# A bidirectional DeltaNet scan in two bursts a step, with split-off diagonal blocks and a written VectorE order

## Chip, core and metric

The kernel runs on one core of a Trainium2 chip. TensorE, VectorE (DVE in the rows), ScalarE (ACT), GpSimd (POOL) and the DMA queues of SyncE (SP), ScalarE and GpSimd work side by side. What counts is the device time of one execution in microseconds (us).

## What is computed

One layer of an encoder on 1024 tokens of width 1024: adaLN, one wide projection, attention beside a bidirectional gated DeltaNet, a merge, and an expert-choice MoE. The change lies in the DeltaNet. Each of its 8 heads cuts the sequence into 16 chunks of 64 tokens, builds a triangular matrix per chunk, inverts it, and scans the chunks forwards and, with other gates, backwards:

```python
L = jnp.where(strict, jnp.einsum('bhncd,bhnsd->bhncs', kb, k) * decay, 0.0)
T = lax.linalg.triangular_solve(eye + L, jnp.broadcast_to(eye, L.shape), left_side=True, lower=True,
                                unit_diagonal=True)
...
def step(state, inp):
    u_n, w_n, a_n, qg_n, kd_n, gl_n = inp
    v_new = u_n - w_n @ state
    o_n = qg_n @ state + a_n @ v_new
    state = state * gl_n[..., None, None] + jnp.einsum('bhck,bhcv->bhkv', kd_n, v_new)
    return state, o_n
```

## The kernel before

The stages follow each other: start and projections of the DeltaNet (to 217 us), matrices of the chunks (`dn_tile`), inversion (`dn_invert`), scan (`scan`, to about 758 us), attention, merge, router and MoE. Wide projections that nothing waits for are spread over the DeltaNet stages to keep TensorE busy: six `qkv_group`s, sixteen gate groups and four `dz` groups, each of 48 matmuls of 128x512 (fp32r, two halves of the operands multiplied in three passes). Their weights are loaded by the GpSimd queue, cast to `wh` by ScalarE (L272) and split to `wl` by VectorE (L273).

**Order.** The builder puts each engine's instructions in an order of its own: it goes by the written order as priority, by when it expects operands to be there, and by which of the buffers of a name (`tr` and `dn` in PSUM, two each; `wh`, `wl`, two each) is free. Inside `manual_schedule(engines={DVE})` VectorE's instructions keep the written order. Before, each of the 31 rounds of the inversion has such a block of its own, so splits and sums may stand between rounds wherever the builder puts them.

**Tiles of a chunk.** `dn_tile(j)` makes, for chunks 2j and 2j+1 and both directions, `at` and `nn` (128x512). `nn` goes to `n_d` in DRAM as 64x64 matrices. `dn_blocks` reads the two 32x32 diagonal blocks of each matrix back into `nb` (one row of 128 partitions for each chunk and head), in rows of 128 bytes and on ScalarE's queue (L508), for tiles 0 to 3 after tile 5 and for the rest after tile 7.

**Inversion.** `dn_invert` needs all of `nb`. It runs 31 rounds of two multiplies (L533) and two subtractions (L537) on VectorE, cut into eight parts between which eight projection groups are written; the blocks' inverses go to `w_d`. In the loop over the groups, `proj_ahead` is called for the next group ahead of the current group's `proj`, and overwrites the entry that this `proj` looks for, so all but the last of these groups load and split their weights twice.

**Scan.** In step t the forward direction treats chunk t, the backward one chunk 15-t; they lie in opposite halves of the 128 partitions. `scan_load` fetches a step's operands, `scan_merge` makes the missing off-diagonal 32x32 block of the inverse (products `pq`, L606, and `pr`, L612, 32x32 matmuls, one quadrant per direction), and `scan_step` does: `pk` (L626, key and query against the state, 128x128), `x = v - pk` on VectorE, `pv` (L638, 64x64 matmuls with the inverse), two scalings to `vb` and `va`, `pu` (L653, the state's update, 64x64), the sum on VectorE and two copies on ScalarE into the state `St`, and `po` (L663, 64x64, the output). A logical fp32 matmul is two instructions in the profile, so a product of 8 heads and two directions is 32. Between these pieces `fill(n)` writes n matmuls of the late projections (L1147, 48 ahead of the first merge). In steps 0 to 7 `attn_prep` (transposes on TensorE, normalisation and rotation on VectorE) runs beside.

Of the kernel before, what the change touches and what calls it, by code (L numbers as in the profile page):

```python
# [20 lines left out]
NT = 8  # L21
# [11 lines left out]
FILL = 12, 10, 4, 4, 8, 48  # L33
# [40 lines left out]
def rev(ap):  # L74

    *dims, (step, n) = [list(x) for x in ap.ap]
    return bass.AP(tensor=ap.tensor, offset=ap.offset + step * (n - 1), ap=dims + [[-step, n]])


class K:  # L80
# [274 lines left out]
    def dn_gates(self, ps):  # L355
# [71 lines left out]
        for t in range(16):  # L427
            for d in range(2):
                n = t if d == 0 else 15 - t
                nc.gpsimd.tensor_copy(gls[:, t, d * 4:d * 4 + 4], gl[:, n // 2, n % 2, d * 4:d * 4 + 4])  # L430
        self.eg, self.gls, self.dk = eg, gls, dk

    def dn_scalars(self):
# [13 lines left out]
        for t in range(16):  # L447
            for d in range(2):
                n = t if d == 0 else 15 - t
                j, x = divmod(n, 2)  # L450
                rows = slice(64 * x, 64 * x + 64)
                nc.gpsimd.tensor_copy(bs[rows, t, 0, :], b2[rows, j, d, :])
                nc.gpsimd.tensor_copy(bs[rows, t, 1, :], b2d[rows, j, d, :])
# [13 lines left out]
    def dn_tile(self, j):  # L467
# [13 lines left out]
        for d in range(2):  # L481
# [17 lines left out]
            for x in range(2):  # L499
                nc.sync.dma_start(self.n_d[d, 2 * j + x].rearrange("h s c -> s h c"),  # L500
                                  nn[64 * x:64 * x + 64].rearrange("p (h c) -> p h c", c=64))

    def dn_blocks(self, j0, j1):

        for d in range(2):
            src = self.n_d[d, 2 * j0:2 * j1].rearrange("n h (b s) c -> (n h) b s c", b=2)
            for b in range(2):
                self.nc.scalar.dma_start(self.nb[d][16 * j0:16 * j1, b], src[:, b, :, b * 32:b * 32 + 32])  # L508

    def dn_invert(self, pool, parts):  # L510
# [13 lines left out]
        for q in range(1, 32):  # L524
            sub = []
            with self.tc.manual_schedule(engines={mybir.EngineType.DVE}):
                for d, (nb, w, tmp) in enumerate(zip(nbs, ws, tmps)):
                    j = 32 - q if d == 0 else q - 1
                    rows = slice(0, j) if d == 0 else slice(j + 1, 32)
                    cols = slice(j, 32) if d == 0 else slice(0, j + 1)  # L530
                    shp = [128, 2, rows.stop - rows.start, cols.stop - cols.start]
                    t = tmp[:, :, rows, cols]
# [3 lines left out]
                for t, u in sub:  # L536
                    nc.vector.tensor_sub(t, t, u)  # L537
# [1087 lines left out]
```

## Time and profile before

| what | value |
|---|---|
| median of 3 runs | 1783.05 us (1782.53 to 1787.27) |
| the profiled execution | 1782.9 us, span 1780.7 us |
| matrices of the chunks | about 217 to 293 us |
| first to last instruction of the inversion | 309.4 to 380.1 us |
| first merge of the scan to the last output of step 15 | 408.9 to about 760 us |
| TensorE busy over the span | 93% |

A row of the timeline gives start, length, engine, line, operation and the names of output and inputs, with the idle time before it and what ended that. A row by stretch gives busy time and number of instructions for each engine, then the granted share of TensorE's clock, the share of time in which the 16 DMA engines were busy, and GB/s.

### The profile page before, as it was taken

To read this page: it belongs to the slowest core of one execution; us is meant where nothing else is said; L and a number is where in the kernel's file an instruction comes from. 1 tells how busy PE (TensorE), PEld (TensorE's weight loads), DVE (VectorE), ACT (ScalarE), POOL (GpSimd) and SP (SyncE) were. 2 spreads that over 40 slices of the span, in tenths; PEclk is the share of its full clock that TensorE was granted. 3 is DMA by queue.
4 is the path that set the end of the run, shared out by engine and by line. 5 is a ranking of instruction groups with operands and counts; after the bars stand their busy time and mean duration, and the time that the engine had idled before them with its cause. 6 is when DMAs were issued, how large, how long until landed. Compare 5 with 4: busy or idle time off the path is not lost. (4 is left out here: it accounts for less than half of the span.)

```text
span 1780.7 us, 28660 instructions
## 1 busy us (share of the span) xinstructions
PE 1663.8 (93%) x10363; PEld 1333.4 (75%) x10363; DVE 1453.2 (82%) x2523; ACT 924.4 (52%) x1372; POOL 256.7 (14%) x287
## 2 busy tenths in 40 slices
PE   6999998389999999999999999939999999999997
PEld 4777876377887778778887778827777777777776
DVE  6899895965777667679998366889999999999997
ACT  5654522113332422268884133327777777777775
POOL 0041512021111100021111212220000110010000
PEclk8999999699999999899999999969999999999999
DMA  9466389256667775431114454569999999999991
GB/s 272 124 178 178 108 214 212 71 174 166 192 188 180 206 224 134 137 124 34 34 35 160 159 204 155 191 238 309 387 387 383 370 384 385 382 373 379 387 335 24
DMA packets 283053, 390.81 MB, mean 219 GB/s; under 512 B 78299, under 2 KB 151695, under 8 KB 282655
## 3 DMA queue, kind: packets, MB, share of 16 engines
q1 hardware_dynamic: 247103, 328.15, 55.5%
q0 software_dynamic: 12960, 47.19, 9.7%
q10 hardware_dynamic: 22848, 13.63, 2.7%
q8 instruction: 82, 1.34, 0.3%
q14 instruction: 60, 0.49, 0.1%
HBM read 330.14 MB, written 58.77 MB: 218 GB/s over the span
## 5 line engine op out<-in xcount | busy, mean ns | idle before, releaser
L1514 DVE TENSOR_TENSOR ew<-er,ew 128x1024 fp32r<-128x1024 f32 x384 | 452.2, 1219 | 30.1 <-ACT ew L1513 30.1
L1513 ACT CAST ew<-er 128x1024 fp32r<-128x1024 f32 x384 | 391.1, 1049 | 138.2 <-PE pj L1567 103.0
L1567 PE MATMUL pj<-ew,xT 128*128 128x512 f32 x1536 | 368.0, 396 | 4.5 <-DVE ew L1514 4.5
L1567 PEld LDWEIGHTS pj<-ew,xT 128*128 128x128 f32 x1536 | 283.3, 188 | 76.4 <-DVE ew L1514 19.5
L1584 PE MATMUL tr<-ew,aT 128*128 128x512 f32 x768 | 191.3, 398 | 0.0
L1584 PEld LDWEIGHTS tr<-ew,aT 128*128 128x128 f32 x768 | 139.7, 188 | 30.5 <-DVE ew L1514 3.5
L279 PE MATMUL pj<-hTh,wl 128*128 128x512 f32 (+1 forms) x368 | 118.6, 401 | 26.4 <-DVE wl L273 26.4
L279 PE MATMUL pj<-hTh,wh 128*128 128x512 f32 (+1 forms) x368 | 118.5, 402 | 3.6 <-ACT hTh L252 1.8
L279 PE MATMUL pj<-hTl,wh 128*128 128x512 f32 (+1 forms) x368 | 118.6, 399 | 1.4 <-DVE hTl L255 1.4
L272 ACT CAST wh<-wraw 128x1024 fp32r<-128x1024 f32 (+1 forms) x45 | 46.7, 1037 | 137.3 <-PE pj L279 66.5
L279 PEld LDWEIGHTS pj<-hTh,wl 128*128 128x128 f32 (+1 forms) x368 | 69.3, 189 | 43.5 <-DVE wl L273 27.0
L1590 POOL DMA_INDIRECT out_dram<-xe,idxT x16 | 37.1, 2317 | 405.6 <-DVE tok L1488 351.1
L269 POOL DMA_DIRECT2D wraw<-in_w_in_dram x42 | 37.7, 898 | 369.4 <-DVE wl L273 278.7
L834 DVE TENSOR_REDUCE am<-pj 128x1 f32<-128x1024 f32 x64 | 77.8, 1217 | 12.4 <-PE pj L829 11.8
L1193 PE MATMUL pj<-hTh,uw 128*128 128x512 f32 x256 | 83.5, 404 | 1.0 <-DVE uth L1199 0.5
L279 PEld LDWEIGHTS pj<-hTh,wh 128*128 128x128 f32 (+1 forms) x368 | 68.6, 190 | 19.8 <-ACT hTh L252 1.9
L1147 PE MATMUL pj<-hTh,wh 128*128 128x512 f32 x240 | 82.7, 412 | 0.0
L1147 PE MATMUL pj<-hTh,wl 128*128 128x512 f32 x240 | 81.9, 410 | 0.0
L279 PEld LDWEIGHTS pj<-hTl,wh 128*128 128x128 f32 (+1 forms) x368 | 68.7, 188 | 17.6 <-DVE hTl L255 2.0
L1147 PE MATMUL pj<-hTl,wh 128*128 128x512 f32 x240 | 81.3, 409 | 0.0
L836 ACT ACTIVATE ap<-pj,am 128x1024 f32<-128x1024 f32 x64 | 71.9, 1123 | 13.9 <-DVE am L834 8.5
L829 PE MATMUL pj<-kT,qT 128*128 128x512 f32 x256 | 77.0, 412 | 1.5 <-ACT ap L836 1.5
(373 smaller groups left out, 3144.5 us busy)
## 6 DMA issues: line engine op xcount, KB each, us to landing
er<-in_w_gate_dram SPq DMA_DIRECT2D x128, 512.0 KB, 7.2
er<-in_w_up_dram SPq DMA_DIRECT2D x128, 512.0 KB
er<-in_w_down_dram SPq DMA_DIRECT2D x128, 512.0 KB, 10.0
wraw<-in_w_in_dram POOLq DMA_DIRECT2D x42, 512.0 KB, 5.8
mw<-in_w_ada_dram SPq DMA_DIRECT2D x64, 256.0 KB, 3.6
wt<-in_w_ada_dram SPq DMA_DIRECT2D x16, 512.0 KB, 8.6
gate_d<-y ACTq DMA_DIRECT2D x32, 256.0 KB, 3.3
kv<-kv_d SPq DMA_DIRECT2D x32, 256.0 KB, 3.6
```

The source lines that it names most:

```text
L269: (queue or nc.gpsimd).dma_start(raw[:, :, :n], self.i["w_in"][0, :, col:col + n].rearrange("(k p) c -> p k c", p=128))
L272: nc.scalar.copy(wh[:, :, :n], raw[:, :, :n])
L279: self.nc.tensor.matmul(ps[q][:n], w[:, k, :n], x[k][:, q * 512:(q + 1) * 512], start=(k == 0 and w is wh and x is self.hTh), stop=(k == 7 ...
L829: nc.tensor.matmul(ps[:, kh], qT[:, i * 128:(i + 1) * 128], self.kT[a][:, s, kh * 512:(kh + 1) * 512], start=(s == 0), stop=(s == 1), skip ...
L834: nc.vector.reduce_max(m, ps, axis=AX.X, negate=True)
L836: nc.scalar.activation(p, ps, AF.Exp, bias=m, scale=1.0, accum_out=self.rv[:, h, half * 4 + i:half * 4 + i + 1])
L1147: nc.tensor.matmul(ps[q], a[:, k], x[k][:, q * 512:(q + 1) * 512], start=(k == 0 and a is wh and x is self.hTh), stop=(k == 7 and a is wl))
L1193: nc.tensor.matmul(ps, w[:, k], v[k][:, qs], start=(k == 0 and p == 0), stop=(k == 3 and p == 2))
L1513: nc.scalar.copy(hi, raw)
L1514: nc.vector.tensor_sub(lo, raw, hi.bitcast(F))
L1567: nc.tensor.matmul(pg[m], x[:, 2 * kp + k], wi[:, k], start=(kp == 0 and k == 0 and n == 0), stop=(kp == 3 and k == 1 and n == 2))
L1584: nc.tensor.matmul(py[q], x[:, k], wi[:, q], start=(k == 0 and n == 0), stop=(k == 7 and n == 2))
```

## The change

- **Scan.** Products of both directions are written head by head, forward and backward in alternation (`pq`, `pr`, `pv`, `pu`, `po`), instead of one direction after the other. `pu` of direction 0 takes a `dn` buffer and that of direction 1 a `tr` buffer. The next step's `scan_merge` is written into the step: its first half ahead of `pv`, its second half behind `po`. The fills stand in four places of 12, 10, 8 and 8. `scan_load` asks for the inverse's blocks first.
- **Diagonal blocks.** `nn` is stored as diagonal blocks in `nb_d` (two SP transfers of 32 rows of partitions for each chunk and direction) and one off-diagonal block in `n_d` (GpSimd's queue). `nb` is then read on SP's queue in rows of 8 KB, two tiles at a time.
- **Inversion.** One `manual_schedule` block holds the whole loop over groups and rounds, so VectorE keeps the written order. One more `proj_ahead` stands behind the last `qkv_group` of the tiles.
- **Gates.** 96 small copies on GpSimd (L430, L452, L453) become 10 strided ones on ScalarE.

```diff
-FILL = 12, 10, 4, 4, 8, 48
+FILL = 12, 10, 8, 8, 48
...
-        for t in range(16):
-            for d in range(2):
-                n = t if d == 0 else 15 - t
-                nc.gpsimd.tensor_copy(gls[:, t, d * 4:d * 4 + 4], gl[:, n // 2, n % 2, d * 4:d * 4 + 4])
+        gl = gl.rearrange("p j x e -> p (j x) e")
+        for d, turn in ((0, lambda a: a), (1, rev1)):
+            nc.scalar.copy(gls[:, :, d * 4:d * 4 + 4], turn(gl[:, :, d * 4:d * 4 + 4]))
...
             for x in range(2):
-                nc.sync.dma_start(self.n_d[d, 2 * j + x].rearrange("h s c -> s h c"),
-                                  nn[64 * x:64 * x + 64].rearrange("p (h c) -> p h c", c=64))
+                n = 2 * j + x
+                rows = lambda b, e: nn[64 * x + 32 * b:64 * x + 32 * b + 32].rearrange(
+                    "p (h c) -> p h c", c=64)[:, :, 32 * e:32 * e + 32]
+                for b in range(2):
+                    nc.sync.dma_start(self.nb_d[d, 8 * n:8 * n + 8, b].rearrange("h s c -> s h c"), rows(b, b))
+                nc.gpsimd.dma_start(self.n_d[d, n].rearrange("h s c -> s h c"), rows(d, 1 - d))
...
-            src = self.n_d[d, 2 * j0:2 * j1].rearrange("n h (b s) c -> (n h) b s c", b=2)
-            for b in range(2):
-                self.nc.scalar.dma_start(self.nb[d][16 * j0:16 * j1, b], src[:, b, :, b * 32:b * 32 + 32])
+            self.nc.sync.dma_start(self.nb[d][16 * j0:16 * j1].rearrange("p b s c -> p (b s c)"),
+                                   self.nb_d[d, 16 * j0:16 * j1].rearrange("n b s c -> n (b s c)"))
...
         pv = self.pa.tile([128, 8, 64], F, name="dn", bufs=2)
-        for r in rs:
-            for h in range(8):
+        for h in range(8):
+            for r in rs:
                 nc.tensor.matmul(pv[r, h], w[r, h], x[r, h], start=True, stop=True, skip_group_check=True)
...
-            for d, r in enumerate(rs):
-                pu = self.pa.tile([128, 4, 64], F, name="dn", bufs=2)
-                for h in range(8):
-                    hb = 64 * (h % 2)
-                    nc.tensor.matmul(pu[hb:hb + 64, h // 2], kv[r, 0, h * 64:h * 64 + 64], vb[r, h],
+            pu = [self.pa.tile([128, 4, 64], F, name=n, bufs=2) for n in ("dn", "tr")]
+            for h in range(8):
+                hr = slice(64 * (h % 2), 64 * (h % 2) + 64)
+                for d, r in enumerate(rs):
+                    nc.tensor.matmul(pu[d][hr, h // 2], kv[r, 0, h * 64:h * 64 + 64], vb[r, h],
                                      start=True, stop=True, skip_group_check=True)
...
             fill(FILL[0])
+            next(merge, None)
             next(step)
             fill(FILL[1])
             some(1)
-            next(step)
+            next(step, None)
+            next(merge, None)
             fill(FILL[2])
-            next(step, None)
-            merge = self.scan_merge(nxt) if nxt else iter(())
-            next(merge, None)
+            some(1)
             fill(FILL[3])
...
+                    if j == QKV[-1]:
+                        self.proj_ahead(C_Q + len(QKV) * 128)
+                    if j in (2, 4, 6):
+                        self.dn_blocks(j - 2, j)
+                self.dn_blocks(6, NT)
```

How the order of instructions changes is shown at three places. The first is TensorE in a step of the scan with attention's preparation beside it. Before (L606 and L612 the merge of the next step, L638 `pv`, L626 `pk`, L143 transposes):

```order
L143 MATMUL tr<-masks,hl 128x128 x4
L606 MATMUL tr<-Sc 32x32 x8
L626 MATMUL dn<-St,kqs 128x128 x4
L1147 MATMUL pj<-hTh_674,wl 128x512
L606 MATMUL tr<-Sc 32x32 x8
L612 MATMUL tr<-W,pt 32x32 x8
L1147 MATMUL pj<-hTh_404,wh 128x512 x2
L143 MATMUL tr<-masks,hl 128x128
L612 MATMUL tr<-W,pt 32x32 x8
```

TensorE at the same place of a step now (L613 and L620 the merge, L635 `pk`, L647 `pv`, L662 `pu`, L149 transposes, L1158 fills):

```order
L1158 MATMUL pj<-hTh_675,wl 128x512
L149 MATMUL tr<-masks,hl 128x128 x4
L662 MATMUL tr<-st,kv 64x64 x8
L1158 MATMUL pj<-hTh_675,wl 128x512
L1158 MATMUL pj<-hTh_405,wh 128x512
L620 MATMUL tr<-W,pt 32x32 x16
L149 MATMUL tr<-masks,hl 128x128 x4
L1158 MATMUL pj<-hTh_405,wh 128x512
L635 MATMUL dn<-St,kqs 128x128 x2
L149 MATMUL tr<-masks,kk 128x128 x4
L635 MATMUL dn<-St,kqs 128x128 x2
```

`pr` has become one run of both directions, as have `pq`, `pv` and `po` elsewhere in the step; `pu` of direction 1 (output `tr`) stands alone, behind the next step's first `pk` and the transposes, while its partner (output `dn`) stays behind `pv`.

The second place is VectorE in the inversion. Before, the second split of weights stands behind 63 rows of rounds and one sum from the first; here it is with its neighbours:

```order
L533 TENSOR_TENSOR wtmp_2847<-nb_708,wb_2843 128x2x16x16
L537 TENSOR_TENSOR wb_2838<-wb_2838,wtmp_2842 128x2x16x16
L537 TENSOR_TENSOR wb_2843<-wb_2843,wtmp_2847 128x2x16x16
L273 TENSOR_TENSOR wl<-wraw,wh 128x1024
L533 TENSOR_TENSOR wtmp_2842<-nb_707,wb_2838 128x2x15x17
```

VectorE at the end of the inversion's second part now (L538 and L542 the rounds, L912 sums of the modulation, L279 splits):

```order
L542 TENSOR_TENSOR wb_2825<-wb_2825,wtmp_2829 128x2x22x10
L542 TENSOR_TENSOR wb_2830<-wb_2830,wtmp_2834 128x2x22x10
L904 TENSOR_TENSOR y<-y,tr 1x512
L912 SCALAR_TENSOR_TENSOR macc<-mw_712,cs,macc 128x512
L912 SCALAR_TENSOR_TENSOR macc<-mw_710,cs,macc 128x512
L279 TENSOR_TENSOR wl<-wraw,wh 128x1024 x2
L538 TENSOR_TENSOR wtmp_2829<-nb_708,wb_2825 128x2x21x11
```

Such a pair of splits now stands behind 24, 40, 52, 64, 76 and 88 of the 124 rows of rounds, with two sums ahead of each. Ahead of the first round there stand three splits among the tiles' last ten of sixteen passes, where there were six, and none of the two that followed the tiles directly.

The third place is the queue that reads `nb`. Before, on ScalarE, behind the last tiles (L272 casts of weights, L889 a cast for the modulation):

```order
L1121 DMA qkv_d<-y 128x512 x2
L272 CAST wh<-wraw 128x1024
L508 DMA nb_707<-n_d 64x32x32 x2
L508 DMA nb_708<-n_d 64x32x32 x2
L889 CAST y<-macc 128x512
```

Now on SP, behind the last tiles (L497 stores of `at`, L507 of diagonal blocks):

```order
L507 DMA nb_d<-nn 32x8x32 x4
L513 DMA nb_708<-nb_d 32x2048
L513 DMA nb_709<-nb_d 32x2048
L497 DMA a_d<-at 128x512
L507 DMA nb_d<-nn 32x8x32 x4
```

The reads have left ScalarE's queue and stand on SP in pairs of 32 rows of partitions; this is the pair of tiles 4 and 5, and only the pair of tiles 6 and 7 stands behind the last store.

## Rows read from the trace of the kernel before

**Rows 1.** The page: the span, and the granted clock in 40 slices.

```profile
span 1780.7 us, 28660 instructions
PEclk8999999699999999899999999969999999999999
```

**Rows 2.** Busy time by stretch: tiles, wait, inversion, fills, scan's two halves.

```profile
220.00:295.00 75.00, 68.99 (x699) 53.84 (x694) 69.36 (x137) 22.69 (x38) 12.67 (x26) 0.95 0.88 222
295.00:309.40 14.40, 14.40 (x65) 11.94 (x64) 1.52 (x5) 1.38 (x3) 5.05 (x4) 1.00 1.05 181
309.40:380.10 70.70, 38.81 (x151) 29.71 (x150) 66.30 (x139) 11.23 (x16) 12.13 (x8) 0.76 0.35 98
380.10:408.90 28.80, 27.48 (x118) 21.69 (x117) 7.30 (x11) 5.03 (x8) 4.82 (x6) 0.98 0.59 193
408.90:590.70 181.80, 178.17 (x1856) 145.32 (x1857) 129.56 (x304) 65.91 (x137) 24.24 (x37) 0.99 0.70 183
590.70:757.60 166.90, 161.70 (x1716) 130.36 (x1712) 113.29 (x250) 45.57 (x97) 6.85 (x7) 0.96 0.64 176
```

**Rows 3.** TensorE's wait in the inversion, and the scan's first merge (timeline).

```profile
343.22 1.22 PE L279 MATMUL pj<-hTh,wl 128*128 128x512 f32 x2 [26.45 <-DVE wl L273]
...
408.90 0.69 PE L606 MATMUL tr<-Sc 32*32 32x32 f32 x16
```

**Rows 4.** VectorE from the last tile to the first round (timeline).

```profile
292.53 0.76 DVE L498 TENSOR_TENSOR nn<-dn,e 128x256 f32<-128x256 f32 x2
...
295.84 1.23 DVE L273 TENSOR_TENSOR wl<-wraw,wh 128x1024 fp32r<-128x1024 f32 x1 [1.42 <-ACT wh L272]
...
309.41 0.28 DVE L533 TENSOR_TENSOR wtmp<-nb,wb 128x62 f32<-128x62 f32 x1 [7.35 <-DMA nb<-n_d]
```

**Rows 5.** TensorE's groups of small matmuls in the scan: busy, mean ns.

```profile
L638 PE MATMUL dn<-st,W 64*64 64x64 f32 x512 | 38.2, 228 | 0.9 <-issue 0.9
L663 PE MATMUL dn<-st,sa 64*64 64x64 f32 x480 | 28.4, 221 | 0.1
L606 PE MATMUL tr<-Sc 32*32 32x32 f32 x512 | 23.0, 195 | 0.0
L612 PE MATMUL tr<-W,pt 32*32 32x32 f32 x512 | 22.7, 195 | 0.0
L653 PE MATMUL dn<-st,kv 64*64 64x64 f32 x480 | 18.5, 224 | 0.0
```

**Rows 6.** Two places with alternating tiles of TensorE (timeline).

```profile
491.96 0.97 PE L653 MATMUL dn<-st,kv 64*64 64x64 f32 x32
...
482.51 0.21 PE L612 MATMUL tr<-W,pt 32*32 32x32 f32 x1
482.54 0.19 PE L606 MATMUL tr<-Sc 32*32 32x32 f32 x1
...
482.63 0.57 PE L612 MATMUL tr<-W,pt 32*32 32x32 f32 x13
```

**Rows 7.** `po` alone (L663), inside a direction, then where directions meet.

```profile
494.30:494.31 0.01, 0.01 (x4) 0.01 (x2) 1.00 0.11 1
...
494.70:494.71 0.01, 0.01 (x7) 0.01 (x4) 1.00 0.00 0
```

**Rows 8.** Busy time in a step with attention's preparation, and one without.

```profile
474.10:497.80 23.70, 23.50 (x243) 19.07 (x242) 17.48 (x43) 8.65 (x18) 2.96 (x5) 1.00 0.66 180
701.00:720.50 19.50, 19.50 (x245) 15.92 (x245) 12.86 (x28) 4.88 (x11) 0.00 (x0) 1.00 0.69 168
```

**Rows 9.** Stretches with a gap on TensorE, and what the clock did.

```profile
597.00:600.00 3.00, 1.26 (x11) 1.04 (x10) 3.00 (x10) 0.27 (x1) 0.00 (x0) 1.00 0.86 236
736.00:742.80 6.80, 4.33 (x28) 3.19 (x27) 6.28 (x20) 1.19 (x2) 0.00 (x0) 1.00 0.49 155
742.80:763.30 20.50, 20.50 (x153) 16.81 (x153) 7.24 (x11) 4.90 (x10) 0.00 (x0) 0.50 0.51 156
```

More of the change, by code (lines that the diff above doesn't have):

```diff
@@ L77, in rev, with rev1 @@
     return bass.AP(tensor=ap.tensor, offset=ap.offset + step * (n - 1), ap=dims + [[-step, n]])
+def rev1(ap):
+    part, (step, n), *dims = [list(x) for x in ap.ap]
+    return bass.AP(tensor=ap.tensor, offset=ap.offset + step * (n - 1), ap=[part, [-step, n], *dims])
 class K:
@@ L446, in dn_scalars @@
         bs = self.ab.tile([128, 16, 2, 8], F, name="bs")
[L447 to L453, printed above, removed]
+        for x in range(2):
+            rows = slice(64 * x, 64 * x + 64)
+            for s, b in enumerate((b2, b2d)):
+                nc.scalar.copy(bs[rows, x::2, s, :], b[rows, :, 0, :])
+                nc.scalar.copy(bs[rows, 1 - x::2, s, :], rev1(b[rows, :, 1, :]))
         self.bs = bs
@@ L525, in dn_invert @@
             sub = []
[L526 to L532, printed above, removed]
-                    nc.vector.tensor_mul(t, nb[:, :, rows, j:j + 1].to_broadcast(shp),
-                                         w[:, :, j:j + 1, cols].to_broadcast(shp))
-                    sub.append((w[:, :, rows, cols], t))
-                for t, u in sub:
-                    nc.vector.tensor_sub(t, t, u)
+            for d, (nb, w, tmp) in enumerate(zip(nbs, ws, tmps)):
+                j = 32 - q if d == 0 else q - 1
+                rows = slice(0, j) if d == 0 else slice(j + 1, 32)
+                cols = slice(j, 32) if d == 0 else slice(0, j + 1)
+                shp = [128, 2, rows.stop - rows.start, cols.stop - cols.start]
+                t = tmp[:, :, rows, cols]
+                nc.vector.tensor_mul(t, nb[:, :, rows, j:j + 1].to_broadcast(shp),
+                                     w[:, :, j:j + 1, cols].to_broadcast(shp))
+                sub.append((w[:, :, rows, cols], t))
+            for t, u in sub:
+                nc.vector.tensor_sub(t, t, u)
             cost += q * (32 - q) + 60
@@ L579, in scan_load @@
         kq, quads = [], []
[L580 to L581 removed]
+        ns = (t, 15 - t)
+        for d, n in enumerate(ns):
             x = n % 2
[L583 removed]
             src = self.w_d[d].rearrange("(n h) (b s c) -> n b s h c", h=8, b=2, s=32)
[L585 removed]
+            nsrc = self.n_d[d, n].rearrange("h s c -> s h c")
             for b in range(2):
@@ L943, in scan @@
             next(step)
+            merge = self.scan_merge(nxt) if nxt else iter(())
             for _ in cur:
```

61 lines of the change are left out of this document (29 added, 32 removed).

## The prediction, written before the change was run

> **What bounds the kernel now.** The page's row of the granted clock is below nine tenths in four of 40 slices, one of them (712 to 757 us) at the scan's end [rows 1]; the clock is not what binds. Then I read the stretches by stage first, since the whole span hides that the DeltaNet stages have different limits. In the scan TensorE is busy 178.2 of 181.8 us and 161.7 of 166.9, VectorE 129.6 and 113.3 [rows 2]: the scan is bound by TensorE's instructions, whether they do much or little. The inversion is the opposite: VectorE is busy 66.3 of 70.7 us, TensorE 38.8 [rows 2], and the reason is one wait of 26.45 us for a split of weights that stands behind 63 rows of rounds [rows 3]. Between tiles and inversion VectorE is almost empty for 14.4 us (1.5 busy) while the DMA engines are full (1.05) [rows 2]; the first round waits for `nb` [rows 4]. The stages behind the scan are untouched and start when it ends, so what is won ahead of them is won for the whole.
>
> **The scan: what alternation is worth.** The five products of a step are 32 instructions each. A step costs TensorE, by busy time over 16 steps (15 where x480) [rows 5]: `pv` 38.2/16 = 2.4 us, `po` 28.4/15 = 1.9, `pq` 23.0/16 = 1.4, `pr` 22.7/16 = 1.4, `pu` 18.5/15 = 1.2. `pu` is cheapest of the three 64x64 products because its heads already alternate between two column halves of the array: a whole run of 32 takes 0.97 us [rows 6], 30 ns each, against 59 for `po`. For 32x32 the trace has one spot where rows of `pr` and `pq` of opposite quadrants interleave: six start between 482.51 and 482.63, 20 ns each [rows 6], against 44 on the average. So two tiles of the array in alternation run at about twice one tile's rate. Priced so, `pv` and `po` cost 1.0 each and `pq` and `pr` 32 x 20 ns = 0.64 plus 0.1 for the start. That saves 1.4 + 0.9 + 0.7 + 0.7 = 3.7 us a step; since a burst's last instruction overlaps what follows it, I use 3.3. `pu` I cost at no change: the order shows its two directions in separate runs in most steps, as now.
>
> The nearest rows bound it: 0 if directions don't overlap, 16 x 3.7 = 59 us if they do and nothing else is late.
>
> What is late next? In a step with attention's preparation VectorE is busy 17.5 of 23.7 us, in one without it 12.9 of 19.5 [rows 8]. The change takes nothing from VectorE. TensorE's share of the first falls to about 23.5 - 3.3 = 20.2, so 2.7 us of VectorE's slack are left, and the order puts `pu` of direction 1 and the copies of its state shortly ahead of the second half of `pk`, with some 2 us of other work between, against a sum on VectorE and two copies on ScalarE. I expect TensorE to wait about 1 us in each of these eight steps, and give up a third of the saving there: 8 x 2.2 + 8 x 3.3 = 44 us. Nothing of it would be 8 x 3.3 = 26, everything 53 to 59.
>
> **The same bank.** A run of `po` is one PSUM tile for both directions. Inside a direction four of its instructions are in flight at once; where direction 0 ends and 1 begins, seven are [rows 7]. So they do overlap across row halves into one tile. The Trainium skill says otherwise: TensorEngine Tiling (Array Packing), Restrictions and Gotchas, states that different row tiles write to different PSUM banks and cannot access the same bank at once. By that, `pq`, `pr`, `pv` and `po` would gain nothing; this is a rival below. The trace disagrees where the directions of `po` meet, for a handful of instructions.
>
> **Tiles and the wait for `nb`.** The last `nn` ends at 293.3 us and the first round starts at 309.4, 16.1 later, 7.35 of it in a wait for `nb` alone [rows 4]. Three splits of 1.2 us (the 295.84 row) leave the tile stage, with one wait of 1.4 like the one shown, so the last `nn` ends near 288. Only 64 rows of `nb` are then still to be stored and read, in 8 KB pieces; before it was 8192 pieces of 128 bytes. I put 7.4 us there, the wait that the row shows (between nothing and 16.1): the first round starts near 295.5. Stores of `nn` grow from 16,384 rows of 256 bytes to 24,576 of 128, and a third of them moves to GpSimd's queue, whose 96 copies are gone; the reads of 16,384 pieces fall to 256, so in sum the engines have less to do, and I cost stores at nothing, covered by a stage in which VectorE is busy 69.4 of 75 us. If that cover fails, the wait of 7.4 becomes 16.1. ScalarE's ten copies are covered too: it is busy 22.7 of 75 [rows 2].
>
> **The inversion.** Of VectorE's 66.3 busy us, six splits (7.3), six sums (4.2) and two additions (1.3) are not rounds [rows 2, 4], so the rounds are about 54. Now twelve splits (14.5), fourteen sums (9.8) and two additions stand between them: 80 us. The splits come in pairs, the first of which is of weights never used; the second gets its `wh` only when the first frees its buffer, so I add the 1.42 us wait of [rows 4] six times: 88 us, to 383.5. Then TensorE: the last pair is split behind 88 of 124 rounds, by the sizes about 72 us after the first round, and from there two groups and the 48 fills are left, 144 x 27.48/118 = 233 ns = 33.5 us [rows 2], plus 1.3 for the modulation's two sums. The first merge starts at 295.5 + 72 + 34.8 = 402, where it was 408.9 [rows 3]: 7 us saved. The 26.45 us wait thus mostly turns into many short ones, as TensorE then keeps step with VectorE. Without the waits for `wh` 12 are saved; with `nb` as late as before, 2 are lost.
>
> **The sum.** 44 + 7 = 51 us off the profiled execution of 1782.9 us (span 1780.7 [rows 1] and 2.2 around it), which stands within 0.2 us of the median, 1783.05: **1732 us**.
>
> **Rivals.**
> *Everything comes off.* The scan gives 56, the inversion 12, and the stretch at half clock behind the gap near 740 us (20.5 us at 0.50, that is 1.2 of 2.4 GHz, worth 10 us [rows 9]) is gone: 1783 - 78 = 1705. For it: TensorE is all but the only limit in the scan. Against it: VectorE's slack in half of the steps.
>
> *VectorE sets the steps with preparation.* Then these eight save nothing, the other eight 26, and the inversion between -2 and +7: 1783 - 26 = 1757. For it: 17.5 of 20.2 us busy, in a fixed order, with waits on both sides [rows 8]. Against it: the same order has cost TensorE 2% before.
>
> *Row halves don't overlap in one bank*, as the skill's rule has it. The scan saves nothing and the inversion 7: 1776. Against it stands [rows 7].
>
> *Slower: short gaps bring the clock down.* A gap of 1.7 us near 598 leaves the clock at 1.00; the gaps of 2.5 us in the stretch to 742.8 are followed by 20.5 us at 0.50 [rows 9]. If the late `pu` of direction 1 makes TensorE wait 2.5 us or more in each step, each costs 2.5 us and at least as much again in half clock (1.7 us for a short spell, 10 for one like that): 16 x 4.2 = 67 us lost against 53 gained, less the inversion's 7 if its gaps do the same: 1797. It decides from about 2.5 us a step; I count 1 us.
>
> **How the numbers follow.** Forecast (1712 to 1745) 0.58; everything 0.12; VectorE sets the steps (1745 to 1768) 0.17; no overlap 0.07; slower 0.06. About 0.3% (5 us) is what a measurement of this kernel can tell from no change. Faster by more: 0.58 + 0.12 + 0.17 and a part of the no-overlap case, 0.90; within it 0.04; slower 0.06. The range 1705 to 1768 leaves out the no-overlap and slower cases and half of the best one, 0.19.
>
> **What the profile of the changed kernel would show.** Right: runs of 32 instructions of `po` and `pv` in about 1 us (L672, L647), of `pq` and `pr` in 0.7; the scan from first merge to last output in about 305 us instead of 350; VectorE busier in the steps with preparation, TensorE with waits of about 1 us at the second half of `pk` (L635) or at the transposes ahead of `pu`; the first merge near 402; the first round 7 to 8 us after the last `nn`; no wait of TensorE over 15 us in the inversion. Wrong: `pv` and `po` still near 2 us (the bank), steps with preparation still over 22 us (VectorE), new stretches at 0.50 in the scan (gaps), or a first merge later than 409.

## The result, and the profile after

The changed kernel takes 1761.74 us (median of 4 runs, 1760.35 to 1764.95), the kernel before 1784.09 beside it: a ratio of 0.9875 (95% interval 0.9854 to 0.9896). Run once more on another chip it gave 0.9899 (0.9861 to 0.9937). So it is faster by 22 us, 1.0 to 1.3%, where 51 us were forecast. The profiled execution took 1760.55 us, its span is 1758.8. The page's span and granted clock:

```profile
span 1758.8 us, 28720 instructions
PEclk9999996799999999999999999969999999999999
```

Slices 7 and 8 (264 to 352 us) now lie below nine tenths, where [rows 1] had only the eighth of them; the dip at the scan's end is gone. The next view is TensorE's timeline (start, length, engine, line, operation, operands, and in brackets the idle time before it and what ended that) in the inversion, at the scan's first merge (L613) and at its last output (L672):

```profile
308.95 1.22 PE L285 MATMUL pj<-hTh,wl 128*128 128x512 f32 x2 [23.51 <-DVE wl L279]
...
333.37 1.22 PE L285 MATMUL pj<-hTh,wl 128*128 128x512 f32 x2 [5.26 <-DVE wl L279]
...
389.40 1.93 PE L285 MATMUL pj<-hTh,wl 128*128 128x512 f32 x3 [4.30 <-DVE wl L279]
...
421.71 0.59 PE L901 MATMUL tr<-y,one 128*1 128x512 f32 x1 [5.27 <-ACT y L898]
...
431.29 0.24 PE L613 MATMUL tr<-Sc 32*32 32x32 f32 x2
...
740.80 1.15 PE L672 MATMUL dn<-st,sa 64*64 64x64 f32 x32
```

The first merge starts at 431.3 us, 22.4 later than before [rows 3], and 29 later than the 402 of the forecast. From there to the last output it is 310.7 us (to 742.0), where it was 352.0 (408.9 to 760.9). What follows takes 1016.8 us instead of 1019.8. So +22.4 - 41.3 - 3.0 = -21.9 us, the difference of the spans: the scan gave nearly what was forecast, and half of that was lost ahead of it. Some 6 of the 41.3 us are the clock's and not the products': by the granted clock of the rows about 21 us of the scan before ran at half clock, 18 of them from 742.8 us on [rows 9], and about 10 us now (the stretches from 431.3 us on, below). With half of these stretches taken off on either side, to have the clock alike, the scan gave some 36 us: an estimate.

Busy time by stretch (columns as in [rows 2]): tiles, TensorE's long wait, inversion in two pieces, the scan's halves.

```profile
220.00:285.40 65.40, 54.11 (x618) 41.48 (x616) 58.37 (x118) 17.98 (x29) 18.92 (x31) 0.91 0.74 182
285.40:309.00 23.60, 0.09 (x2) 0.05 (x1) 14.72 (x43) 0.00 (x0) 6.76 (x7) 0.50 0.47 113
309.00:389.40 80.40, 64.20 (x249) 49.40 (x249) 54.00 (x86) 16.93 (x22) 10.48 (x11) 0.86 0.43 128
389.40:431.30 41.90, 36.49 (x139) 28.23 (x139) 21.71 (x49) 5.04 (x8) 6.58 (x8) 0.87 0.58 178
431.30:590.70 159.40, 153.86 (x1771) 122.23 (x1771) 125.24 (x293) 61.49 (x130) 23.63 (x36) 0.98 0.76 198
590.70:742.00 151.30, 146.99 (x1840) 116.00 (x1839) 118.17 (x263) 50.50 (x105) 8.29 (x8) 0.99 0.74 202
```

From 309.0 to 389.4 VectorE is busy 54.0 of 80.4 us, where it had been busy 66.3 of 70.7 [rows 2]: VectorE, which bounded the inversion, now waits in it. Its timeline says for what (L501 the last `nn`, L538 rounds, L279 splits, L904 the modulation's sum, which adds a bias to a product of TensorE, L901):

```profile
289.30 0.76 DVE L501 TENSOR_TENSOR nn<-dn,e 128x256 f32<-128x256 f32 x2 [0.49 <-DVE e L498]
...
297.12 0.26 DVE L538 TENSOR_TENSOR wtmp<-nb,wb 128x62 f32<-128x62 f32 x1 [1.81 <-DMA nb<-nb_d]
...
306.54 2.35 DVE L279 TENSOR_TENSOR wl<-wraw,wh 128x1024 fp32r<-128x1024 f32 x2
...
328.92 0.67 DVE L904 TENSOR_TENSOR y<-y,tr 1x512 f32<-1x512 f32 x1 [12.31 <-DMA y<-in_b_ada_dram]
...
386.09 0.67 DVE L904 TENSOR_TENSOR y<-y,tr 1x512 f32<-1x512 f32 x1 [10.56 <-DMA y<-in_b_ada_dram]
...
388.13 2.35 DVE L279 TENSOR_TENSOR wl<-wraw,wh 128x1024 fp32r<-128x1024 f32 x2
```

The two waits ahead of L904 are 22.9 us. The releaser named, the load of the bias, is the event that came last by the records; what it needs is a chain: the group's last matmul, its output copied and stored, a buffer `y` free (there are two, and the bias goes into one as well), ScalarE's L898 and GpSimd's L899, the product L901 on TensorE. On TensorE L901 stands behind all 48 matmuls of a group. ScalarE's row shows the middle of the chain, a copy that waited for the group's output to be stored:

```profile
325.24 0.62 ACT L898 CAST y<-macc 128x512 fp32r<-128x512 f32 x1 [1.61 <-DMA qkv_d<-y]
```

While VectorE waits for it TensorE works, and then TensorE waits 5.3 and 4.3 us for the splits that stand behind L904 in VectorE's written order: the two engines take turns. The granted clock is low in these stretches too, 0.86 and 0.87 in the rows above.

TensorE's groups of small products in the scan (busy, mean ns, idle before), to be read beside [rows 5]:

```profile
L647 PE MATMUL dn<-st,W 64*64 64x64 f32 x512 | 23.5, 223 | 0.3 <-DVE oss L694 0.3
L672 PE MATMUL dn<-st,sa 64*64 64x64 f32 x512 | 20.0, 227 | 4.5 <-issue 4.5
L613 PE MATMUL tr<-Sc 32*32 32x32 f32 x512 | 12.8, 193 | 0.0
L620 PE MATMUL tr<-W,pt 32*32 32x32 f32 x512 | 11.2, 192 | 0.6 <-PE tr L662 0.6
L662 PE MATMUL dn<-st,kv 64*64 64x64 f32 x240 | 10.9, 225 | 0.6 <-DVE st L652 0.6
L662 PE MATMUL tr<-st,kv 64*64 64x64 f32 x240 | 10.4, 224 | 0.0
```

One instruction is as long as before (223 ns for `pv`, 228 before); more of them are in flight at once.

### The profile page after: what moved, and what is told of

It reads as the page before. It is cut to its first block, busy times and chain, and to the rows that moved or that the text cites. A ratio compares the mean times of both kernels' runs of the same rounds, so it can differ in the third digit from the quotient of the medians.

```text
span 1758.8 us, 28720 instructions
## 1 busy us (share of the span) xinstructions
PE 1625.8 (92%) x10363; PEld 1292.5 (73%) x10363; DVE 1456.3 (83%) x2524; ACT 926.6 (53%) x1383; POOL 234.0 (13%) x224
## 5 line engine op out<-in xcount | busy, mean ns | idle before, releaser
L1578 PEld LDWEIGHTS pj<-ew,xT 128*128 128x128 f32 x1536 | 283.2, 188 | 76.2 <-DVE ew L1525 19.5
L1158 PE MATMUL pj<-hTh,wl 128*128 128x512 f32 x240 | 83.6, 415 | 0.0
L1158 PE MATMUL pj<-hTl,wh 128*128 128x512 f32 x240 | 82.9, 415 | 0.0
L1158 PE MATMUL pj<-hTh,wh 128*128 128x512 f32 x240 | 82.1, 412 | 0.1
```

The source lines that it names most:

```text
L1158: nc.tensor.matmul(ps[q], a[:, k], x[k][:, q * 512:(q + 1) * 512], start=(k == 0 and a is wh and x is self.hTh), stop=(k == 7 and a is wl))
L1578: nc.tensor.matmul(pg[m], x[:, 2 * kp + k], wi[:, k], start=(kp == 0 and k == 0 and n == 0), stop=(kp == 3 and k == 1 and n == 2))
```

## The experiments

All ratios are to the kernel before, run on the same chip beside them.

### One direction after the other again

```diff
-        for h in range(8):
-            for r in rs:
+        for r in rs:
+            for h in range(8):
                 nc.tensor.matmul(pv[r, h], w[r, h], x[r, h], start=True, stop=True, skip_group_check=True)
```

and likewise for `pq`, `pr` and `po` in the changed kernel; the rest of the change stays.

> The changed kernel, but pq, pr, pv and po are written one direction after the other, as before the change; the two bursts, the places of the fills and the split of pu stay. Theory A: the alternation alone carries the scan's gain of 41 us; the scan (first merge to last output) goes from 311 back to 350 us or a little more, and the time is 1798 to 1810, slower than before the change. Rival D: the gain comes from the two bursts and the moved fills, at least by half: the time is 1762 to 1782.

1791.6 us, 1.0056 (1.0035 to 1.0077): slower than before the change. The scan takes 346.0 us. The same groups of products:

```profile
L647 PE MATMUL dn<-st,W 64*64 64x64 f32 x512 | 36.9, 224 | 0.0
L672 PE MATMUL dn<-st,sa 64*64 64x64 f32 x512 | 32.6, 229 | 0.9 <-issue 0.9
L613 PE MATMUL tr<-Sc 32*32 32x32 f32 x512 | 19.7, 192 | 0.0
L620 PE MATMUL tr<-W,pt 32*32 32x32 f32 x512 | 17.5, 192 | 0.0
```

106.7 us of busy time against 67.5 with alternation. Theory A holds, though 30 us came back by the median and 35 by the scan's length, somewhat less than the 36 to 48 expected.

### Alternation alone, in the kernel before

The same four loops turned round in the kernel before, and nothing else.

> The kernel before, with nothing but the alternation of directions in pq, pr, pv and po. Theory A: alternation alone carries the scan's gain, wherever the products stand: the scan (352 us from first merge to last output) shortens by 33 to 42 us and the time is 1738 to 1750, which is faster than the whole change. Rival D: the gain needs the two bursts and their places, since shorter products leave TensorE waiting for the merge at the end of a step: less than half is won, 1760 to 1775.

1737.1 us, 0.9743 (0.9726 to 0.9759): this one part gives 45 us, twice what the whole change gives. The scan takes 309.0 us, all of it at a granted clock of 1.00. With the two bursts, the moved fills and the `tr` buffer of `pu` it is 310.7 at 0.98, so these add little: some 3 us with the clock alike, in one trace of each. TensorE's long wait in the inversion is as in [rows 3]:

```profile
339.65 1.22 PE L279 MATMUL pj<-hTh,wl 128*128 128x512 f32 x2 [25.35 <-DVE wl L273]
```

### The written order alone, in the kernel before

```diff
+                with self.tc.manual_schedule(engines={mybir.EngineType.DVE}):
                     for n, (f, c, g) in enumerate(fills):
...
-            with self.tc.manual_schedule(engines={mybir.EngineType.DVE}):
                 for d, (nb, w, tmp) in enumerate(zip(nbs, ws, tmps)):
```

> The kernel before with one part of the change only: VectorE's written order over the whole inversion. Theory A: this part is what costs the inversion 22 us: the sum of the modulation again holds VectorE for some 20 us behind TensorE's group, the first merge comes at 420 to 435 instead of 408.9 and the time is 1792 to 1808. Rival J: the cost needs the other parts (diagonal blocks, one more load ahead); alone the written order gives as much by an earlier split as it takes: 1776 to 1788.

1799.83 us, 1.0082 (1.0052 to 1.0112): slower. The first merge starts at 429.9; it is a cleaner measure than the time, which holds a spell of half clock in the scan (shown in the last section). VectorE's timeline (here L532 is a round, L894 the sum):

```profile
295.60 0.26 DVE L532 TENSOR_TENSOR wtmp<-nb,wb 128x62 f32<-128x62 f32 x1 [6.22 <-DMA nb<-n_d]
...
328.31 0.67 DVE L894 TENSOR_TENSOR y<-y,tr 1x512 f32<-1x512 f32 x1 [11.75 <-DMA y<-in_b_ada_dram]
...
385.35 0.68 DVE L894 TENSOR_TENSOR y<-y,tr 1x512 f32<-1x512 f32 x1 [10.45 <-DMA y<-in_b_ada_dram]
```

This part alone makes both waits (22.2 us) and moves the first merge by 21.0 us: theory A. It also starts the rounds at 295.6 where they started at 309.4 [rows 4], with the old blocks and their old transfers.

### The sum written one pass later

The changed kernel, with L904 and its store held back until the next pass of the loop has written its rounds.

```diff
-            nc.vector.tensor_add(mb, mb, ps[0:1])
-            nc.sync.dma_start(self.mod_d[row:row + 1, qs], mb)
+                self.hold.append((mb, ps, row, qs))
...
+                        held, self.hold = self.hold or [], []
                         mod(MODS[1])
+                        self.mod_sums(held)
```

> The changed kernel with its written order, but the modulation's sum and its store are written one pass of the loop later (behind the next group's rounds). Theory A: the two waits of VectorE for it (12.3 and 10.6 us) shrink to under 2 us each, the first merge comes about 21 us earlier (near 410), and the time is 1738 to 1743; the third such wait, ahead of the scan on TensorE, may stay (5 us). Rival B (too much work on VectorE, or TensorE bound there): the wait moves to something else and less than 6 us are won, 1755 to 1762.

1750.51 us, 0.9841 (0.9803 to 0.9879), which overlaps the changed kernel's interval. Both waits of VectorE are gone (no gap over 2.74 us among the rounds), and the first merge starts at 418.8, 12.5 us earlier, not 21: between theory A and rival B. What limits it now is TensorE: from its first group to the first merge it is busy 96.5 of 109.4 us.

```profile
309.40:418.80 109.40, 96.52 (x387) 75.17 (x388) 78.00 (x134) 22.02 (x30) 20.77 (x20) 0.93 0.53 159
```

So the two waits account for 12.5 of the 22.4 us lost at the first merge. Behind them stood TensorE's own work: seven groups and the 48 fills, 384 matmuls, at the 233 ns of the prediction 89.5 us, all of it behind 309, as TensorE still stands idle until then.

### The long order taken back to single rounds

```diff
+            with self.tc.manual_schedule(engines={mybir.EngineType.DVE}):
                 for d, (nb, w, tmp) in enumerate(zip(nbs, ws, tmps)):
...
-                with self.tc.manual_schedule(engines={mybir.EngineType.DVE}):
                     for n, (f, c, g) in enumerate(fills):
```

> The changed kernel, but VectorE's written order holds only inside each of the 31 rounds of the inversion, as before the change. Theory A: the first merge comes at 431 us instead of the predicted 402 because the long written order puts the modulation's sum (L904, it waits for a product that TensorE makes behind a whole group) ahead of splits and rounds; without it no wait of VectorE over 5 us is left between the rounds, the first merge comes about 95 to 105 us after the first round, as before the change (so near 397 to 405), and the time is 1727 to 1738. Rival B: VectorE simply has too much to do there (pairs of splits, half of them of weights never used, and their waits for the cast): the first merge stays at 420 or later and the time within 1752 to 1765.

1746.9 us, 0.9814 (0.9785 to 0.9843), between the two theories. The first merge starts 91.5 us after the first round, somewhat less than theory A's 95 to 105, but the first round starts at 322.7 and not at 297: three splits with their waits for casts stand ahead of it, and the tiles themselves end at 304.8. The long order buys an early start and pays for it with the waits; the price was higher. TensorE still waits, four times for 3 us or more; three of them:

```profile
329.28 1.22 PE L285 MATMUL pj<-hTh,wh 128*128 128x512 f32 x2 [8.40 <-ACT y L1131]
...
368.73 0.58 PE L902 MATMUL tr<-y,one 128*1 128x512 f32 x1 [10.79 <-POOL y L900]
...
372.55 1.93 PE L285 MATMUL pj<-hTh,wl 128*128 128x512 f32 x3 [3.24 <-DVE wl L279]
```

### Weights kept for their group

```diff
-        self.ahead = col, self.proj_load(col)
+        self.ahead[col] = self.proj_load(col)
...
-        if self.ahead and self.ahead[0] == col:
-            wh, wl = self.ahead[1]
-            self.ahead = None
-        else:
-            wh, wl = self.proj_load(col, n)
+        wh, wl = self.ahead.pop(col, None) or self.proj_load(col, n)
```

> The changed kernel, but weights loaded ahead are kept for the group that they are for, so each group's weights are split once (seven loads, casts and splits less). Theory A: TensorE then has a group's weights one pass early and runs it beside the rounds, so the sum L904 finds its product nearly done and its waits shrink from 12.3 and 10.6 to under 6; with 14 us less of splits and of waits for casts the first merge comes near 395 to 405, the time is 1725 to 1737. Rival B: only the splits go (7 x 1.2 us and 6 x 1.1 us of waits, 15 us at most), the waits for L904 stay: first merge 415 to 420, time 1745 to 1752.

1726.0 us, 0.9691 (0.9665 to 0.9717). The first merge starts at 395.0. The stretch of TensorE's long wait, and from its end to the first merge:

```profile
306.60:395.00 88.40, 86.71 (x369) 70.55 (x370) 71.71 (x132) 15.59 (x23) 11.46 (x12) 0.97 0.49 152
285.00:306.60 21.60, 0.00 (x1) 0.00 (x1) 13.71 (x43) 0.00 (x0) 6.46 (x8) 0.58 0.47 108
```

TensorE is busy without a wait over 1.7 us from 306.6 on. With a group's split one pass ahead, TensorE has work while VectorE runs rounds, L904 finds its product made, and of the two waits one of 5.6 us is left among the rounds. Theory A in full: by rival B's price, 15 us at most, fewer splits and waits for casts could not have done it.

### Two groups ahead

```diff
-                        if n + 1 < len(fills):
-                            with self.tc.high_priority(offset=0):
-                                self.proj_ahead(fills[n + 1][1] + fills[n + 1][2] * 128)
                         f(g)
+                        if n + 2 < len(fills):
+                            self.proj_ahead(fills[n + 2][1] + fills[n + 2][2] * 128)
```

with the first of them ahead of the loop, and weights kept.

> The changed kernel with weights that are loaded ahead kept, and written two groups ahead, so that one more split stands ahead of the first round. In the kernel with weights kept only, TensorE still stood idle for 21.7 us (284.9 to 306.6) for a split that stands behind the first part of the rounds, though VectorE itself waited for nb until then, and from there to the first merge TensorE had no wait over 1.8 us. Theory A: TensorE's start after the tiles is now what sets the first merge: it comes 8 to 17 us earlier than 395 (378 to 387, bounded by the end of the rounds and the way of the inverse through DRAM), and the time is 1708 to 1719. Rival E: VectorE's rounds set it after all (they ended at 376 there): under 4 us are won, 1721 to 1727.

1726.31 us, 0.9675 (0.9656 to 0.9694): the same as the kernel above within the intervals. TensorE's timeline behind the tiles, and the first merge:

```profile
301.10 1.22 PE L285 MATMUL pj<-hTh,wh 128*128 128x512 f32 x2 [4.95 <-ACT y L1127]
...
311.50 1.22 PE L285 MATMUL pj<-hTh,wl 128*128 128x512 f32 x2 [8.32 <-DVE wl L279]
...
393.49 0.24 PE L609 MATMUL tr<-Sc 32*32 32x32 f32 x2
```

TensorE works until 296 instead of 285, but then waits again for a split behind the first part of the rounds. The long wait was cut in pieces and moved, the first merge came 1.5 us earlier instead of 8 to 17. The early split alone does not hold TensorE: theory A's reason was too simple. Time and first merge are rival E's, and the rounds end at 376.0 us as they do without the edit; but TensorE works without a wait of 0.8 us or more from 311.5 to the first merge, so which of the two engines sets it stays open.

### Weights kept, order of single rounds

Both edits at once on the changed kernel, and, as the second run, keeping the weights in the kernel before with alternation.

> The changed kernel with weights kept and VectorE's written order only inside each round. Without keeping, this order let the tiles run to 304.8 and the first round start at 321.6, as splits and sums came ahead of them. Theory A: with six or seven splits less the tiles end near 292, the first merge comes near 390 and the time is 1715 to 1726, no worse than with weights kept and the long written order (1726). Rival I: without the long written order the rounds start late whatever the splits are (after 312): the first merge after 400 and 1732 to 1747.

> The kernel before with the alternation of directions and with weights kept for the group that they are loaded for; the inversion's rounds stay in blocks of one round. With the alternation alone TensorE still waited 25.3 us in the inversion for a split that stood behind half of the rounds, and the first merge came at 404.9. Theory A: each group's weights are then split once and one group ahead, so that wait is gone and six splits with it: the first merge comes at 385 to 397 and the time is 1717 to 1730. Rival H: the wait comes from where the builder puts a split among rounds, not from the doubled ones: 402 or later and 1732 to 1738.

1733.47 us, 0.9742 (0.9703 to 0.9782), and 1737.66 us, 0.9742 (0.9698 to 0.9785). Together with the others this makes a table of ratios:

| kernel | weights loaded twice | kept |
|---|---|---|
| the change, long written order | 0.9875, 0.9899 | 0.9691 |
| the change, order of single rounds | 0.9814 | 0.9742 |
| before with alternation, single rounds | 0.9743 | 0.9742 |

The order's effect turns its sign: with weights loaded twice it costs, with weights kept it gains. Keeping them is worth some 35 us beside the long order, 13 beside single rounds, and nothing in the kernel before, where the builder puts the remaining splits as late as it put the doubled ones (TensorE's wait there is still 15.0 us, the first merge at 405.3: rival H). That the order gains beside kept weights rests on 0.9691 (0.9665 to 0.9717) against 0.9742 (0.9703 to 0.9782), intervals that overlap a little. In the first of the two kernels the first merge comes at 401.0, as rival I has it. TensorE waits 19.5 us there for the modulation's product, and GpSimd's row shows an operation of 1.3 us that took 19.7:

```profile
340.40 19.74 POOL L896 TENSOR_TENSOR y<-macc,y 128x512 fp32r<-128x512 f32 x1 [25.71 <-DMA gate_d<-y]
```

```profile
360.20 0.59 PE L898 MATMUL tr<-y,one 128*1 128x512 f32 x1 [19.55 <-POOL y L896]
```

### That subtraction on VectorE

```diff
-            nc.gpsimd.tensor_sub(lo, acc, hi.bitcast(F))
+            nc.vector.tensor_sub(lo, acc, hi.bitcast(F))
```

in both kernels with the order of single rounds, weights kept and weights loaded twice.

> The changed kernel with weights kept and VectorE's written order only inside each round, and with the modulation's one small subtraction (ahead of the product that the sum waits for) on VectorE instead of GpSimd. Without this last edit it took GpSimd 19.7 us beside VectorE's rounds instead of 1.3, until VectorE paused, and TensorE waited 19.5 us for it. Theory K: GpSimd can't get at its operands while VectorE works without a pause; on VectorE the subtraction takes 0.7 us, TensorE's wait falls under 4 us, the first merge comes 10 to 17 us earlier (384 to 391) and the time is 1715 to 1724. Rival L: what TensorE waits for is ready late for another reason (the buffer y, the builder's order): the wait stays above 10 us on another engine's instruction, 1729 to 1738.

> The changed kernel with VectorE's written order only inside each round and that subtraction on VectorE; weights still loaded twice. Without the last edit TensorE waited 10.8 us for it. Theory K: that wait falls under 4 us and the first merge comes 6 to 9 us earlier than 414, the time is 1735 to 1742 where it was 1747. Rival L: no change, 1743 to 1750.

1734.64 us, 0.9747 (0.9722 to 0.9772), and 1754.68 us, 0.9857 (0.9837 to 0.9877). Neither is faster than without the edit (0.9742 and 0.9814), though the first merge comes 5 and 6 us earlier (395.7 for 401.0, 408.2 for 414.2). In the second kernel the scan takes that back and more: 321.2 us at a granted clock of 0.96, where it was 309.4 at 0.99; so the order of single rounds is then no better than the long one (0.9875). On VectorE the subtraction takes 0.67 us, but TensorE's wait remains, in the first kernel for a split, in the second for the subtraction itself, which stands behind rounds in VectorE's order:

```profile
350.25 1.22 PE L285 MATMUL pj<-hTh,wl 128*128 128x512 f32 x2 [11.78 <-DVE wl L279]
```

```profile
365.22 0.59 PE L902 MATMUL tr<-y,one 128*1 128x512 f32 x1 [10.17 <-DVE y L900]
```

Theory K's forecast fails: both waits stay over 10 us, which is rival L's sign in the first kernel. Slow GpSimd was the last in a row of causes: with single rounds the builder lets the rounds run ahead of small operations that TensorE waits for, and in both kernels another of them stepped in when this one was taken away.

### The old diagonal blocks

The changed kernel with `n_d`, the stores and the reads of `nb` as before.

> The changed kernel with the diagonal blocks stored and read as before the change (whole 64x64 matrices on SP, nb read in rows of 128 bytes on ScalarE's queue, tiles 0 to 3 behind tile 5 and the rest at the end). Theory A: the first round waits for nb again, 14 to 17 us after the last nn instead of 7, so it starts at 304 to 309 instead of 297; as splits stand behind the first part in written order, TensorE and the first merge move by the same 7 to 12 us, and the time is 1767 to 1775. Rival F: the long written order has other waits that take up the delay: within 3 us of the changed kernel, 1758 to 1765.

1764.2 us, 0.9895 (0.9878 to 0.9912), a ratio between the two of the changed kernel (0.9875 and 0.9899). The first rounds:

```profile
298.78 0.26 DVE L535 TENSOR_TENSOR wtmp<-nb,wb 128x62 f32<-128x62 f32 x1 [6.13 <-DMA nb<-n_d]
301.97 0.26 DVE L535 TENSOR_TENSOR wtmp<-nb,wb 128x62 f32<-128x62 f32 x1 [2.93 <-DMA nb<-n_d]
```

Both directions' first rounds have `nb` at 302.0, 3 us later than the 298.9 of the changed kernel, not 7 to 12. Rival F: the blocks make no difference that these runs can tell.

### `pu` as one run

The kernel written two groups ahead, with TensorE's written order around the loop of `pu`.

> As the kernel that is written two groups ahead, and TensorE's 32 instructions of pu held in written order, so that its two directions alternate instead of standing in two runs of 16 (0.61 us each in the changed kernel). Once in the changed kernel the 32 stood together and took 0.52 us, 16 ns each, as four tiles of the array alternated. Theory A: 0.5 to 0.7 us a step come off, 8 to 10 us against the kernel without this: 1700 to 1710. Rival G: direction 0 now waits until a PSUM buffer of the other name is free, the state is ready later and TensorE waits at the next pk: no gain or up to 10 us slower than that kernel.

1729.25 us, 0.9704 (0.9681 to 0.9727), against 0.9675 without: no gain, which is the time that rival G gives. Runs of `pu` with 16 ns an instruction do appear in nearly every step. Where the gain went is not shown: TensorE's waits at `pk` are 3.4 us in sum, 3.0 without the edit, so rival G's own place does not carry it; ahead of the merge they are 6.4 instead of 3.4:

```profile
L609 PE MATMUL tr<-Sc 32*32 32x32 f32 x512 | 13.3, 198 | 6.4 <-issue 6.2 <-DVE Sc L606 0.2
```

### The changed kernel again

> The changed kernel itself once more, on the same chip as the three others, to compare them with it directly: 1756 to 1766, a ratio to before of 0.985 to 0.990.

1762.39 us, 0.9899 (0.9861 to 0.9937), as expected.

## Why the prediction was right and wrong

- **TensorE bounds the scan, and alternation pays: right in mechanism, too large in size.** 44 us were forecast for the scan and 41.3 came, but some 6 of these are half clock that went away, which the sum left out (it stands in the case "everything comes off" alone). With the clock alike some 36 came; by the same reckoning taking the alternation out again cost 31 us of scan, and alternation alone gave 32. The four products cost 67.5 us of busy time where they had cost 114.2 (38.2 + 23.0 + 22.7, and 28.4 scaled from 480 to 512 [rows 5]): 2.9 us a step, priced at 3.7 and used as 3.3. A run of 32 `po` takes 1.15 us (the row at 740.80; 1.0 priced, 1.9 before).
- **`pu` at no change: slightly off.** Its two separate runs take 21.3 us in sum, where they took 18.5 [rows 5].
- **VectorE holds a part back in the steps with preparation: not shown.** From output to output steps 1 to 7 took 160.0 us and take 147.0, 1.9 us a step for the 2.2 used (one of them below, to be read beside [rows 8]: VectorE busy 16.9 of 20.6 us). The last eight went from 168.4 to 143.1, 3.2 a step for the 3.3, but that this fits is luck: about 18 of the 168.4 us ran at half clock [rows 9], and about 3 of the 143.1. With the clock alike both kinds of step gave a little over 2 us, so the 3.3 of the last eight was half as much again as came.

```profile
458.36:478.97 20.61, 20.55 (x240) 16.22 (x239) 16.88 (x42) 8.01 (x18) 3.74 (x6) 1.00 0.82 204
```

- **One PSUM bank: the rival is refuted.** The Trainium skill (TensorEngine Tiling (Array Packing), Restrictions and Gotchas) has it that different row tiles cannot access one bank at once. The runs differ from it: `pv` and `po` alternate between two row halves that write different partitions of one PSUM tile of 2 KB a partition, a run of `po` takes 1.15 us for 1.9, and the kernel before with alternation alone is 45 us faster. That is what [rows 7] had shown for a handful of instructions.
- **First round near 295.5: right in time, wrong in cause.** It started at 297.1, 7.1 us after the last `nn`. But with the old blocks it starts within 2 to 5 us of that, and with the written order alone at 295.6. So the new blocks, to which the step gave the larger part, matter little. VectorE was almost idle in the 16 us of [rows 4], too: the last four reads of `nb` took 13.9 us to issue on ScalarE's queue, beside two loads of weights (512 KB each, issued at 294.7 and 297.4 behind splits). In the kernel before with the written order alone the same reads have no such load beside them and take 5.7 us. That the loads slow the reads was not tried apart. The reads before, and with the written order:

```profile
294.91 13.87 ACTq L508 DMA_DIRECT2D nb<-n_d  x4
...
288.74 5.74 ACTq L508 DMA_DIRECT2D nb<-n_d  x4
```

- **The inversion saves 7 us: wrong, it lost 22.4.** This is the step that failed. The prediction's chain was: first round, 72 us of VectorE to the last pair of splits, 34.8 us of TensorE to the first merge, 402. Measured: 297.1 (+1.6), the last pair done at 390.5, 93.4 later (+21.4), then 40.8 us (+6.0, of which 5.3 is TensorE's wait at 421.71). Without the two waits for L904 the 93.4 would be 70.5, so the work was priced well and the wait was missing. With these waits written away the first merge still comes at 418.8: the other 9.9 of the 22.4 us are TensorE's, which does nothing from 285.4 to 309 and then has 384 matmuls to do. The sums were counted as work, "fourteen sums (9.8)", and nothing was asked about what a sum waits for. In the order of VectorE shown ahead of the prediction L904 stands three rows above the two splits, with `tr`, a PSUM buffer, as its input: it was there to be seen. The wait of 26.45 us did not turn "into many short ones"; it became two long ones on VectorE and several on TensorE. Of the prediction's signs of being wrong, the first merge later than 409 came.
- **"No wait of TensorE over 15 us": wrong.** It waits 23.5 us from 285.4 on. The three splits that left the tiles were counted as relief for VectorE. For TensorE they were the weights of the groups that it had run there: in the stretch in which it was busy 14.4 of 14.4 us [rows 2] it now stands still.
- **Rivals.** The measured 1761.7 us lies inside the stated range of 1705 to 1768, by luck: the case there was "VectorE sets the steps with preparation" (1757), and its mechanism is not what happened. No rival had a wait of VectorE in its new written order, although the change adds just such an order.

What is settled: the written order, beside weights that are loaded twice, makes the loss (21.0 us by itself in the kernel before); the waits for the modulation's sum carry 12.5 of the 22.4 us in the changed kernel, and keeping the weights undoes all of it. Not settled is what would be left if TensorE were given work from 285 us on, since none of these kernels did that in full. The copies of the gates, the one more `proj_ahead`, the order of `scan_load` and a third buffer `y` were not tried apart. The fastest version run, the change with weights kept, is at 1726 us, 3.1% under the kernel before and 2% under the change.

## What to carry to other kernels

Where an engine gets a written order, price each row by what it waits for, above all small rows that read PSUM: an engine that waits in order passes its wait to all that stands behind it, and here 22.9 us hung on two rows of 0.67. Where a change takes work off a busy engine, ask who lived on its results; and test the parts of a change apart, since one of them was worth twice the whole. Before a forecast counts as right, compare the granted clock of the two stretches: here 6 of 41 us were the clock's.

## What the runs showed of the hardware

- Tiles of TensorE's array in alternation run side by side, also into one PSUM tile: 32 instructions of 64x64 took 1.15 us in two row halves, where one half after the other took 1.9 [rows 5]. Four tiles (two halves each of rows and columns, into two PSUM tiles) start one about every 16 ns (32 within 0.48 us), as at the one place in the changed kernel where all 32 of `pu` stand together:

```profile
618.06 0.22 PE L662 MATMUL dn<-st,kv 64*64 64x64 f32 x1
618.07 0.22 PE L662 MATMUL tr<-st,kv 64*64 64x64 f32 x1
618.08 0.22 PE L662 MATMUL dn<-st,kv 64*64 64x64 f32 x1
618.08 0.22 PE L662 MATMUL tr<-st,kv 64*64 64x64 f32 x1
```

- A gap was followed by a spell of half clock that cost several times its length. In the kernel before with the written order TensorE waited 3.7 us from 594.6 on; the granted clock fell to 0.50 at 596.7 and stayed there for 30.7 us, although TensorE was busy 29.1 of them (its timeline, then the stretch):

```profile
598.33 1.62 PE L625 MATMUL dn<-St,kqs 128*128 128x128 f32 x6 [3.72 <-DMA kqs<-kq_d]
```

```profile
596.70:627.40 30.70, 29.07 (x209) 23.02 (x210) 10.09 (x23) 7.84 (x16) 1.78 (x3) 0.50 0.60 151
```

  In the changed kernel's group from 333.4 us on, a pair of matmuls starts every 0.85 us at 0.50 and every 0.46 us at full clock, so the 29.1 us of work would take about 16, and the spell costs some 13 us: an estimate.
- GpSimd's subtraction of 128x512 takes 1.3 to 1.8 us in nearly all places, and 4.8 to 19.7 in six places where VectorE runs rounds without a pause; the longest ended 1.1 us after VectorE paused. The Trainium skill (SBUF — State Buffer, Who interferes with whom) says that a VectorE instruction with two SBUF inputs contends with a GpSimd instruction that reads SBUF. The durations agree; that the page's port is the cause was not tried apart, and moving the subtraction did not shorten the kernel.
